# A hybrid conv/gMLP decoder layer in five matmul units: conv taps leave each unit's last row pair, y and z rows are prepared one pair sooner

## The chip, the cores and the metric

The kernel runs on one core of one Trainium2 chip. The metric is the device time of one execution in microseconds (us). The kernel before takes 1897.69 us (median of 3 runs, 1892.99 to 1901.14).

## The reference

The layer takes x of 4096 rows by 1024 columns in float32. Cut to what matters:

```python
h = layer_norm(x, ln_emb_g, ln_emb_b)
a_val, a_gate, a_z, b_u, b_v, b_z = split(h @ w_in, 6)          # 512 columns each
a = a_val * sigmoid(a_gate)
a = causal_depthwise_conv(a, conv_w, conv_b)                     # 31 taps per channel, along the rows
y_a = silu(layer_norm(a, conv_ln_g, conv_ln_b)) * silu(a_z)
v = layer_norm(gelu(b_v), sgu_ln_g, sgu_ln_b)                    # in chunks of 128 rows
sv = einsum("hts,bcshd->bcthd", tril(w_s), v) + b_s              # 8 heads, lower-triangular 128 x 128
y_b = gelu(b_u) * sv * silu(b_z)
z = layer_norm(ALPHA * h + concat(y_a, y_b) @ w_out, post_ln_g, post_ln_b)
out = z + sigmoid(z @ w_ple_gate + b_ple_gate) * (p @ w_ple)
```

## The kernel before

**Five units.** The work is five 1024 x 1024 products over all 4096 rows, one after the other, each called a unit: unit(0) makes a_val and a_gate, unit(1) b_u and b_v, unit(2) b_z and a_z, unit(3) the product with `w_out`, unit(4) the gate. The words of the change count them from one: its fourth unit is unit(3), its fifth unit(4). A unit runs over 16 pairs of 128 rows (`for p in range(NP)`, L427). A pair is one call of `group` (L325): a Strassen-like scheme that needs seven products of quarter blocks instead of eight, each product 12 matmuls of 128 x 512 (four blocks of the inner dimension, each as high times high, high times low, low times high part; L312 to L314). So a pair is 84 matmuls into the PSUM banks pa, pb, pd, pe. A VectorE or ScalarE instruction called `plus` (L328) moves an intermediate from one bank to another between the products, and TensorE cannot write the bank again before that instruction has read it.

**What is made beside the products.** For a product, a left operand is split into a high part (`ahi`, ScalarE, L231) and the rest (`alo`, POOL or VectorE, L232). A weight is loaded (`wst`, L414), and split into `whi` (ScalarE, L172) and `wlo` (VectorE, L173) in two halves; a unit has seven weights, thus 14 `wlo` instructions of 128 x 1024. The weights of the next unit are loaded and split during the last pair of a unit. In unit(3) and unit(4) the left operands come from rows that are first transposed by TensorE (`rows_left`, L245). The rows of y (L669) need a LayerNorm with six POOL instructions per pair (L691, L692, L694), the rows of z (L753) two multiplies and two adds of 128 x 1024 with the LayerNorm's gain and bias `prow`. The convolution (L365) runs on VectorE as 47 instructions, called taps here, for each of 16 blocks of 128 channels by 1024 rows; each tap reads one SBUF tile and a PSUM accumulator (L386, L392, L395).

**What sets the order.** The program is written with generators that are advanced a few steps at each of six places within a pair (`between`, L437): `bg` makes the left operands of the next pair, `bg_x` the rows of a later one, `bg_w` the weights, `bg_post` what follows a pair, and `bg_conv` the taps. At places 2 and 3 of every pair `bg_conv.step(conv_quota)` lets the quota of taps go: 6 in unit(0), 6 in unit(1), 10 in unit(2), 5 in unit(3), thus twice that in a pair. The order in which an engine's instructions finally stand is then set by the framework's scheduler; after that each engine works strictly in order, as does the queue of SP, which issues every DMA. A DMA whose data or buffer is not ready holds all later ones in SP's queue.

**Buffers.** Seven `big` buffers (8 KB per partition) hold weights in flight (`wst`), left operands before the split (`qa`, `qb`), rows of y, z and h, conv results (`cz`) and, from the end of unit(3) on, the pair of rows `prow`. Two `ca` buffers hold the convolution's input; after it they hold the bias row `gb` and the staging of `w_ple` (`wps`).

Of the kernel before, what the change touches and what calls it, by code (L numbers as in the profile page):

```python
# [8 lines left out]
F32 = mybir.dt.float32  # L9
# [3 lines left out]
ADD, SUB, MUL = ALU.add, ALU.subtract, ALU.mult  # L13
# [18 lines left out]
NP = S // (2 * P)  # L32
# [32 lines left out]
def hybrid_layer_kernel(  # L65
# [27 lines left out]
    pool = ctx.enter_context(tc.tile_pool(name="pool", bufs=1))  # L93
# [5 lines left out]
    def big(shape, name, dt=F32):  # L99
        return pool.tile(shape, dt, tag="big", name=name, bufs=7)  # L100
# [38 lines left out]
    def pair(t):  # L139
        return t.rearrange("j p d -> p j d")  # L140
# [35 lines left out]
    def combos(u):  # L176


        for c in range(4):
            q = big([P, 4, C], "bq")  # L180
            for i in range(2):
                for j in range(2):
                    dma(q[:, 2 * i + j], wq[u, i, j][:, c])
            yield
            for n, k in ((1, 0), (2, 2), (3, 3)):
                dma(twD[u][ROW[n]][:, c], q[:, k])
            ptt(q[:, 0], q[:, 1], q[:, 0], op=SUB)
            dma(twD[u][ROW[5]][:, c], q[:, 0])
            yield
            ptt(q[:, 1], q[:, 3], q[:, 1], op=SUB)  # L190
            dma(twD[u][ROW[7]][:, c], q[:, 1])
            yield
            ptt(q[:, 3], q[:, 3], q[:, 0], op=SUB)
            dma(twD[u][ROW[6]][:, c], q[:, 3])
            yield
            ptt(q[:, 2], q[:, 2], q[:, 3], op=SUB)
            dma(twD[u][ROW[4]][:, c], q[:, 2])
            yield
# [30 lines left out]
    def left(src, eng):  # L229
        hi, lo = atile("ahi"), atile("alo")  # L230
        act(hi, src, ID)  # L231
        eng.tensor_tensor(lo, src, hi.bitcast(F32), op=SUB)  # L232
        return hi, lo

    def left_kept(p, L):

        qa, qb = big([P, 4, C], "qa"), big([P, 3, C], "qb")
        dma(qa, qD[p][:, 0:4])
        dma(qb, qD[p][:, 4:7])
        yield  # L240
        for i, n in enumerate(ORDER):
            L[n] = left(quad((qa[:, i] if i < 4 else qb[:, i - 4])), nc.gpsimd)
            yield
# [162 lines left out]
    bg_x = Background()  # L406
    bg_w = Background()
    bg_conv = Background()
    bg_post = Background()

    def load_operands(u, W):
        for n in ORDER:
            stg = big([P, 4, C], "wst")
            dma(stg, twD[u][ROW[n]])  # L414
            W[n] = split_weight(stg)
            yield

    def broadcast(src, n, name, tile_of=big):
        t = tile_of([P, n, src.shape[-1]], name)
        for i in range(n):  # L420
            dma(t[:, i], src[i : i + 1, :].partition_broadcast(P))
        return t

    def unit(u, L, W, next_left, next_first, body, conv_quota, lag=0):


        for p in range(NP):  # L427
            Lnext, Wnext = {}, {}
            last = p + 1 == NP
            if not last:  # L430
                bg.add(next_left(p + 1, Lnext))
            elif next_first is not None:
                bg.add(next_first(Lnext))
                bg_w.drain()
                bg_w.add(load_operands(u + 1, Wnext))

            def between(i):  # L437
                bg_x.step(2 if lag else 1)
                if i >= lag:
                    bg.step(3 if lag else 2)  # L440
                bg_post.step(2)
                if last and u + 1 < 5:
                    bg_w.step(2 if i == 5 else 1)
                else:
                    bg_w.step(1)
                if i in (2, 3):
                    with tc.issue_after(anchor[0].ins):
                        bg_conv.step(conv_quota)

            body(p, L, W, between)  # L450
            bg.drain()
            bg_x.drain()
            if last:
                bg_w.drain()
                W = Wnext
            L = Lnext
        return L, W
# [39 lines left out]
    W = {}  # L497
# [4 lines left out]
    L = {}  # L502
# [51 lines left out]
    L, W = unit(0, L, W, left_a, lambda L: left_kept(0, L), body_a, 6)  # L554
# [65 lines left out]
        if p % 2 == 1:  # L620
            bg_post.add(mix(p // 2, V["g"], V["h"], V["l"]))

    L, W = unit(1, L, W, left_kept, lambda L: left_kept(0, L), body_b, 6)
    bg_post.drain()


    def body_c(p, L, W, between):
        if p == 1:
            bg_w.add(combos(3))
        if p == NP - 3:  # L630
            for i in range(2):
                cgb.append(broadcast(crow[i : i + 1, :], 1, "cgb", utile))
            load_y(0)
        elif p >= NP - 2:
            bg_x.add(y_rows(p - NP + 2))
        ua = big([P, 2, 2, C], "ua")
        us, az = ua[:, 0], ua[:, 1]
        dma(us, pair(uD[p // 2][2 * (p % 2) : 2 * (p % 2) + 2]))
        pa, pd = group(L, W, None, az[:, 0], az[:, 1], between)
        act(az, az, AF.Silu)  # L640
        dma(pair(azD[p]), az)
        for j, ps in ((0, pa), (1, pd)):
            zz = utile([P, C], "zz")
            act(zz, ps, AF.Silu)
            ptt(us[:, j], us[:, j], zz, op=MUL)
        dma(pair(ybD[p]), us)
        if p == NP - 2:
            load_y(1)
        elif p == NP - 1:
            load_h(0)  # L650
            load_y(2)
# [17 lines left out]
    def y_rows(p):  # L669
        cz, y = CZ.pop(p), Y[p]  # L670
        cc = flat(cz[:, 0]).rearrange("p (c j x) -> p c j x", c=CT, j=2)
        for j in (1, 0):
            tp = sbank("tc")
            for ct in range(CT):
                nc.tensor.transpose(
                    out=tp[:, ct * P : (ct + 1) * P],
                    in_=cc[:, ct, j],
                    identity=ident,
                )
            act(y[:, j, 0:C], tp, ID)  # L680
        yield
        mv = mvtile(2)
        for j in (1, 0):
            moments([y[:, j, 0:C]], mv[:, j, :])
        nb = scale_bias(mv)
        yield
        for j in (1, 0):
            ya = y[:, j, 0:C]
            act(ya, ya, ID, scale=mv[:, j, 1:2], bias=nb[:, j : j + 1])
            yield  # L690
            ptt(ya, ya, cgb[0][:, 0], op=MUL)  # L691
            ptt(ya, ya, cgb[1][:, 0], op=ADD)  # L692
            act(ya, ya, AF.Silu)
            ptt(ya, ya, cz[:, 1, j], op=MUL)  # L694
            yield

    def left_y(p, L):
        return rows_left(L, Y.pop(p))
# [2 lines left out]
        H[p] = big([P, 2, D], "hr")  # L701
        dma(H[p], pair(hT[p]))

    L, W = unit(2, L, W, left_kept, lambda L: left_y(0, L), body_c, 10)


    def z_out(p, z):
# [12 lines left out]
    def body_d(p, L, W, between):  # L720
        if p == 1:
            bg_w.add(combos(4))
        h = H.pop(p)
        if p + 1 < NP:
            load_h(p + 1)
        if p + 2 < NP:
            bg_x.add(y_rows(p + 2))
        if p + 2 >= NP:
            bg_x.add(z_rows(p + 2 - NP))
        z = big([P, 2, D], "z")  # L730
        pa, pd = group(
            L, W, [h[:, 0, 0:C], h[:, 0, C:], h[:, 1, 0:C], h[:, 1, C:]],
            z[:, 0, C:], z[:, 1, C:], between, scale=ALPHA,
        )
        for j, ps in ((0, pa), (1, pd)):
            act(z[:, j, 0:C], ps, ID)
        bg_post.drain()
        bg_post.add(z_out(p, z))
        if p + 3 < NP:
            load_y(p + 3)  # L740
        elif p + 3 == NP:
            pb_.append(broadcast(prow, 2, "prow"))
            load_z(0)
        elif p + 2 == NP:
            load_z(1)

    Z = {}

    def load_z(p):
        Z[p] = big([P, 2, D], "zr")  # L750
        dma(Z[p], pair(zT[p]))

    def z_rows(p):  # L753
        for j in (1, 0):
            ptt(Z[p][:, j], Z[p][:, j], pb_[0][:, 0], op=MUL)  # L755
            ptt(Z[p][:, j], Z[p][:, j], pb_[0][:, 1], op=ADD)  # L756
            yield

    pb_ = []
# [4 lines left out]
    def first_z(L):  # L764
        yield from left_z(0, L)

    L, W = unit(3, L, W, left_y, first_z, body_d, 5, 2)
    bg_post.drain()


    def row_tile(name):
        return pool.tile([P, D], F32, tag="ca", name=name, bufs=2)

    gb = row_tile("gb")
    dma(gb, grow.partition_broadcast(P))
    wp_hi, wp_lo = big([P, 2, D], "wph", F32R), big([P, 2, D], "wpl", F32R)

    def split_wp():
        for k in range(2):
            wps = row_tile("wps")  # L780
            dma(wps, wp[k])
            act(wp_hi[:, k], wps, ID)
            tt(wp_lo[:, k], wps, wp_hi[:, k].bitcast(F32), op=SUB)
# [105 lines left out]
```

## Time and profile before

| | |
|---|---|
| median of 3 runs | 1897.69 us |
| the profiled execution's own time | 1898.2 us |
| its span, first to last instruction | 1896.5 us |
| mean granted TensorE clock | 0.986 |
| busy share of the span: TensorE matmul / VectorE / POOL / ScalarE | 95% / 75% / 67% / 47% |
| DMA | 363.62 MB, mean 192 GB/s |

TensorE (PE) is busy nearly throughout, VectorE (DVE) and POOL for most of the time, and the DMA queues have room. The 92.5 us in which PE is idle (1896.5 less 1804.0 busy) are not spread evenly. The page cuts the span into 40 slices of 47 us and gives each engine's busy share in tenths. To see a stage more closely one asks for stretches. The pairs are found in the trace by counting matmuls, 84 to a pair: unit(1) starts at 401.06 us, unit(2) at 749.08, unit(3) at 1072.51, unit(4) at 1449.54. The stretches below run from the first matmul of one pair to the first of the next, so that their length is what the pair costs. In a stretch's row stand its length, then for each engine the busy us and the number of instructions, then the granted clock, the DMA share and the DMA rate.

### The profile page before, as it was taken

What the parts mean: (1) busy time and instruction counts of PE and PEld (TensorE: products, weight loads), DVE (VectorE), ACT (ScalarE), POOL (GpSimd) and SP (SyncE); (2) the same over time, 40 slices, a digit from 0 to 9 for tenths busy, and PEclk for the clock granted to TensorE, in tenths of its full rate; (3) what the DMA queues carried; (4) which work ended last, traced back from release to release, by engine and by line L of the source; (5) the groups of instructions that cost most, each with busy time, mean ns of one, the idle gap of its engine ahead of it and who ended that gap; (6) DMA issues with size and microseconds to landing.
All of it is one profiled execution on the core that took longest, in us unless ns stands there. A gap on an engine that the chain in (4) does not pass through costs nothing. (4 is left out here: it accounts for less than half of the span.)

```text
span 1896.5 us, 24392 instructions
## 1 busy us (share of the span) xinstructions
PE 1804.0 (95%) x8322; PEld 1470.9 (78%) x8322; DVE 1413.6 (75%) x2176; ACT 892.4 (47%) x1438; POOL 1269.9 (67%) x1015
## 2 busy tenths in 40 slices
PE   4799999999999999999999899999999999999999
PEld 3687788877788887788888677787887787888887
DVE  8637877797787778978787998887558856665654
ACT  4655555565455555544444634445555422332222
POOL 2878987458777676588668568757676856655541
PEclk9899999999999999999999889999999999999999
DMA  6579776586734445898666758745555322222311
GB/s 239 195 236 359 248 235 206 194 287 211 239 124 147 139 142 173 302 358 298 211 198 227 272 186 284 242 150 191 197 189 220 119 95 78 89 90 95 100 54 52
DMA packets 184940, 363.62 MB, mean 192 GB/s; under 512 B 49648, under 2 KB 74224, under 8 KB 177136
## 3 DMA queue, kind: packets, MB, share of 16 engines
q1 hardware_dynamic: 184816, 362.07, 55.3%
q8 instruction: 66, 1.08, 0.2%
q14 instruction: 58, 0.48, 0.1%
HBM read 211.02 MB, written 150.99 MB: 191 GB/s over the span
## 5 line engine op out<-in xcount | busy, mean ns | idle before, releaser
L232 POOL TENSOR_TENSOR alo<-s,ahi 128x512 fp32r<-128x512 f32 x192 | 262.8, 1382 | 260.7 <-ACT ahi L231 252.9
L312 PE MATMUL pb<-whi,ahi 128*128 128x512 f32 x960 | 385.9, 402 | 18.3 <-ACT pa L330 5.2
L313 PE MATMUL pb<-wlo,ahi 128*128 128x512 f32 x960 | 378.4, 394 | 1.6 <-DVE wlo L173 1.6
L314 PE MATMUL pb<-whi,alo 128*128 128x512 f32 x960 | 378.4, 394 | 0.1
L312 PE MATMUL pe<-whi,ahi 128*128 128x512 f32 x640 | 258.9, 405 | 19.6 <-ACT ahi L231 8.5
L314 PE MATMUL pe<-whi,alo 128*128 128x512 f32 x640 | 256.6, 401 | 2.1 <-POOL alo L232 2.1
L313 PE MATMUL pe<-wlo,ahi 128*128 128x512 f32 x640 | 254.6, 398 | 4.2 <-DVE wlo L173 4.2
L312 PEld LDWEIGHTS pb<-whi,ahi 128*128 128x128 f32 x960 | 182.3, 190 | 63.6 <-ACT pa L330 8.8
L314 PEld LDWEIGHTS pb<-whi,alo 128*128 128x128 f32 x960 | 182.1, 190 | 39.5 <-POOL alo L232 0.6
L313 PEld LDWEIGHTS pb<-wlo,ahi 128*128 128x128 f32 x960 | 182.7, 190 | 38.4 <-DVE wlo L173 2.6
L232 POOL TENSOR_TENSOR alo<-qa,ahi 128x512 fp32r<-128x512 f32 x128 | 171.2, 1353 | 48.1 <-ACT ahi L231 47.8
L231 ACT ACTIVATE ahi<-s 128x512 fp32r<-128x512 f32 x192 | 119.7, 629 | 138.9 <-DVE s L284 54.6
L386 DVE SCALAR_TENSOR_TENSOR acc<-ca,cs_sb,acc 128x512 f32<-128x512 f32 x240 | 180.1, 750 | 4.3
L395 DVE SCALAR_TENSOR_TENSOR acc<-ca,cw_sb,acc 128x512 f32<-128x512 f32 x240 | 179.0, 746 | 0.1
L392 DVE SCALAR_TENSOR_TENSOR acc<-zy,cw_sb,acc 128x512 f32<-128x512 f32 x224 | 166.8, 745 | 1.2 <-POOL zy L378 0.4
L312 PEld LDWEIGHTS pe<-whi,ahi 128*128 128x128 f32 x640 | 122.7, 192 | 47.1 <-ACT ahi L231 10.3
L232 POOL TENSOR_TENSOR alo<-qb,ahi 128x512 fp32r<-128x512 f32 x96 | 126.8, 1329 | 39.2 <-ACT ahi L231 38.2
L313 PEld LDWEIGHTS pe<-wlo,ahi 128*128 128x128 f32 x640 | 122.6, 191 | 30.4 <-DVE wlo L173 6.5
L232 DVE TENSOR_TENSOR alo<-tp,ahi 128x512 fp32r<-128x512 f32 x144 | 98.2, 683 | 62.9 <-ACT ahi L231 60.5
L314 PEld LDWEIGHTS pe<-whi,alo 128*128 128x128 f32 x640 | 122.3, 191 | 27.8 <-POOL alo L232 3.3
L312 PE MATMUL pd<-whi,ahi 128*128 128x512 f32 x320 | 129.4, 404 | 4.4 <-ACT pd L330 3.2
L159 POOL TENSOR_TENSOR mv<-mv,nhalf 128x2 f32<-128x2 f32 (+1 forms) x81 | 55.2, 687 | 111.2 <-DVE mv L158 110.3
(151 smaller groups left out, 4006.7 us busy)
## 6 DMA issues: line engine op xcount, KB each, us to landing
qa<-qD SPq DMA_DIRECT2D x32, 1024.0 KB, 6.5
twD<-bq SPq DMA_DIRECT2D x112, 256.0 KB, 5.7
wst<-twD SPq DMA_DIRECT2D x28, 1024.0 KB, 6.9
qb<-qD SPq DMA_DIRECT2D x32, 768.0 KB, 6.8
xr<-in_x SPq DMA_DIRECT2D x32, 512.0 KB, 5.4
hT<-xr SPq DMA_DIRECT2D x32, 512.0 KB, 3.8
qD<-s SPq DMA_DIRECT2D x64, 256.0 KB, 2.9
bq<-in_wq SPq DMA_DIRECT2D x64, 256.0 KB, 5.2
```

The source lines that it names most:

```text
L159: ptt(mv[:, :, 1], mv[:, :, 1], nhalf[:, 0:n], op=ALU.pow)
L231: act(hi, src, ID)
L232: eng.tensor_tensor(lo, src, hi.bitcast(F32), op=SUB)
L312: nc.tensor.matmul(ps, lhsT=ah[:, k, :], rhs=wh[:, k, :], start=start and k == 0, stop=False, **kw)
L313: nc.tensor.matmul(ps, lhsT=ah[:, k, :], rhs=wl[:, k, :], start=False, stop=False, **kw)
L314: nc.tensor.matmul(ps, lhsT=al[:, k, :], rhs=wh[:, k, :], start=False, stop=k == 3, **kw)
L386: stt(even, src, w, even, op0=MUL, op1=ADD)
L392: stt(dst, src, cw_sb[:, ct, 2 * k + 1 : 2 * k + 2], odd if k else even, op0=MUL, op1=ADD)
L395: stt(src if k == NE - 1 else even, src, cw_sb[:, ct, 2 * k : 2 * k + 1], even, op0=MUL, op1=ADD,)
```

## The change

Four things change, and with them the order on every engine.

1. `between` no longer lets taps go in the last pair of a unit. The quotas rise by one to make up for it: 7 in unit(1), 11 in unit(2), 6 in unit(3); unit(0) stays at 6.
2. In unit(2) the loads of y rows 0 and 1 and their preparation move one pair towards the front: `load_y(0)` and the `cgb` rows from the start of pair 13 to pair 12, `y_rows(0)` and `y_rows(1)` from pairs 14 and 15 to 13 and 14.
3. In unit(3) both `load_z(0)` and `load_z(1)` stand at the end of pair 13; `z_rows(0)` stays in pair 14 on POOL, `z_rows(1)` moves from pair 15 to pair 14 and from POOL to VectorE.
4. `prow` is loaded at pair 10 as two rows into the `ca` buffers, and `gb` and `wps` go to `big` buffers instead.

```diff
-                if i in (2, 3):
+                if i in (2, 3) and not last:
                     with tc.issue_after(anchor[0].ins):
                         bg_conv.step(conv_quota)
...
-    L, W = unit(1, L, W, left_kept, lambda L: left_kept(0, L), body_b, 6)
+    L, W = unit(1, L, W, left_kept, lambda L: left_kept(0, L), body_b, 7)
...
-        if p == NP - 3:
+        if p == NP - 4:
             for i in range(2):
                 cgb.append(broadcast(crow[i : i + 1, :], 1, "cgb", utile))
             load_y(0)
-        elif p >= NP - 2:
-            bg_x.add(y_rows(p - NP + 2))
+        elif p in (NP - 3, NP - 2):
+            bg_x.add(y_rows(p - NP + 3))
...
-        if p == NP - 2:
+        if p == NP - 3:
             load_y(1)
...
-    L, W = unit(2, L, W, left_kept, lambda L: left_y(0, L), body_c, 10)
+    L, W = unit(2, L, W, left_kept, lambda L: left_y(0, L), body_c, 11)
...
-        if p + 2 >= NP:
-            bg_x.add(z_rows(p + 2 - NP))
+        if p == 10:
+            for i in range(2):
+                pb_.append(row_tile("prow"))
+                dma(pb_[i], prow[i : i + 1, :].partition_broadcast(P))
+        if p + 2 == NP:
+            bg_x.add(z_rows(0))
+            bg_post.add(z_rows(1, nc.vector))
...
         elif p + 3 == NP:
-            pb_.append(broadcast(prow, 2, "prow"))
             load_z(0)
-        elif p + 2 == NP:
             load_z(1)
...
-    def z_rows(p):
+    def z_rows(p, eng=nc.gpsimd):
         for j in (1, 0):
-            ptt(Z[p][:, j], Z[p][:, j], pb_[0][:, 0], op=MUL)
-            ptt(Z[p][:, j], Z[p][:, j], pb_[0][:, 1], op=ADD)
+            eng.tensor_tensor(Z[p][:, j], Z[p][:, j], pb_[0], op=MUL)
+            eng.tensor_tensor(Z[p][:, j], Z[p][:, j], pb_[1], op=ADD)
             yield
...
-    L, W = unit(3, L, W, left_y, first_z, body_d, 5, 2)
+    L, W = unit(3, L, W, left_y, first_z, body_d, 6, 2)
...
-    gb = row_tile("gb")
+    gb = big([P, D], "gb")
...
-            wps = row_tile("wps")
+            wps = big([P, D], "wps")
```

The scheduler's order, counted pair by pair on VectorE (from one `L355` to the next), has these taps. Last pair of unit(0) and first of unit(1): 11 and 9 before, 6 and 6 now. Last of unit(1) and first of unit(2): 12 and 8, now 8 and 2. Pairs 14 and 15 of unit(2) and pair 0 of unit(3): 19, 16 and 14, now 21, 10 and 10. Pairs 1 to 10 of unit(3): 14, 11, 12, 8, 11, 12, 8, 12, 10, 1, now 8, 13, 10, 14, 15, 12, 2, 0, 0, 0. Pairs 1 to 14 of unit(1) hold 172 taps before and 196 now, pairs 1 to 14 of unit(2) 285 and 314. In unit(4)'s first pair the bias instruction `pa<-pb,gb`, without which TensorE can't go on in bank pb, stands behind 8 of the 14 `wlo` halves before and behind 13 now, and the load of `gb` behind the seventh weight's in SP's queue.

On VectorE, at the last pair of unit(2), where the weights of unit(3) are split (`wlo`) between taps (L386, L392, L395), before:

```order
L355 TENSOR_TENSOR ua<-pb,s_9619 128x512
L386 SCALAR_TENSOR_TENSOR acc<-ca,cs_sb,acc 128x512 x4
L173 TENSOR_TENSOR wlo<-wst,whi 128x1024
L392 SCALAR_TENSOR_TENSOR acc<-zy,cw_sb,acc 128x512
L395 SCALAR_TENSOR_TENSOR acc<-ca,cw_sb,acc 128x512
L173 TENSOR_TENSOR wlo<-wst,whi 128x1024
L392 SCALAR_TENSOR_TENSOR acc<-zy,cw_sb,acc 128x512
L274 TENSOR_TENSOR s_9843<-tp,a_9836 128x512
L395 SCALAR_TENSOR_TENSOR acc<-ca,cw_sb,acc 128x512
L392 SCALAR_TENSOR_TENSOR acc<-zy,cw_sb,acc 128x512
L395 SCALAR_TENSOR_TENSOR acc<-ca,cw_sb,acc 128x512
L392 SCALAR_TENSOR_TENSOR acc<-zy,cw_sb,acc 128x512
```

and at the same place now:

```order
L355 TENSOR_TENSOR ua<-pb,s_9692 128x512
L395 SCALAR_TENSOR_TENSOR ca<-ca,cw_sb,acc 128x512
L386 SCALAR_TENSOR_TENSOR acc<-ca,cs_sb,acc 128x512 x2
L173 TENSOR_TENSOR wlo<-wst,whi 128x1024
L386 SCALAR_TENSOR_TENSOR acc<-ca,cs_sb,acc 128x512
L173 TENSOR_TENSOR wlo<-wst,whi 128x1024
L386 SCALAR_TENSOR_TENSOR acc<-ca,cs_sb,acc 128x512
L274 TENSOR_TENSOR s_9911<-tp,a_9904 128x512
L386 SCALAR_TENSOR_TENSOR acc<-ca,cs_sb,acc 128x512
L173 TENSOR_TENSOR wlo<-wst,whi 128x1024
L386 SCALAR_TENSOR_TENSOR acc<-ca,cs_sb,acc 128x512
L173 TENSOR_TENSOR wlo<-wst,whi 128x1024
```

Fewer taps stand between the `wlo` halves, and the third and fourth half have moved up.

On SP's queue at the end of unit(1), where unit(2)'s weights (`wst`) are loaded; `cD` are the stores of a finished convolution block, which wait for its last taps, before:

```order
L239 DMA qb<-qD_109 128x1536
L414 DMA wst<-twD_174 128x2048
L401 DMA cD_130<-zy 1024x1x64
L414 DMA wst<-twD_174 128x2048
L401 DMA cD_130<-ca 1024x1x64
L414 DMA wst<-twD_174 128x2048
L375 DMA ca<-aD_126 128x2x15
L376 DMA ca<-aD_127 128x2x512
L414 DMA wst<-twD_174 128x2048 x4
```

and now:

```order
L401 DMA cD_130<-zy 1024x1x64
L401 DMA cD_130<-ca 1024x1x64
L375 DMA ca<-aD_126 128x2x15
L376 DMA ca<-aD_127 128x2x512
L238 DMA qa<-qD_109 128x2048
L239 DMA qb<-qD_109 128x1536
L586 DMA uD_139<-g_6582 128x4x512
L414 DMA wst<-twD_174 128x2048 x7
```

The conv block's stores have moved ahead of the weights, whose seven loads now stand together behind one other store (`uD`).

On VectorE in pair 14 of unit(3), where `pa` and `u` are the instructions that free bank pb, before:

```order
L334 SCALAR_TENSOR_TENSOR s_13288<-hr,pe 128x512
L334 SCALAR_TENSOR_TENSOR pa<-hr,pb 128x512
L232 TENSOR_TENSOR alo<-tp,ahi 128x512
L334 SCALAR_TENSOR_TENSOR u_13315<-hr,pb 128x512
L274 TENSOR_TENSOR s_13347<-tp,a_13340 128x512
```

and now, with line numbers of the changed kernel (L761 and L762 are the z rows' multiply and add):

```order
L334 SCALAR_TENSOR_TENSOR s_13291<-hr,pe 128x512
L761 TENSOR_TENSOR zr<-zr,prow 128x1024 x2
L232 TENSOR_TENSOR alo<-tp,ahi 128x512
L334 SCALAR_TENSOR_TENSOR pa<-hr,pb 128x512
L762 TENSOR_TENSOR zr<-zr,prow 128x1024 x2
L334 SCALAR_TENSOR_TENSOR u_13318<-hr,pb 128x512
```

Four instructions of 128 x 1024 have come in, two in front of each instruction that frees bank pb.

## Rows read from the trace of the kernel before

**Rows 1.** Busy tenths in 40 slices of the span, PE and VectorE.
```profile
PE   4799999999999999999999899999999999999999
DVE  8637877797787778978787998887558856665654
```

**Rows 2.** Stretches by pair, unit(2) pairs 13 to 15, unit(3) pair 0.
```profile
1007.97:1027.01 19.04, 19.04 (x86) 15.77 (x84) 15.12 (x24) 9.34 (x17) 15.91 (x14) 1.00 0.58 195
1027.01:1047.86 20.85, 20.85 (x101) 17.42 (x100) 17.47 (x28) 10.70 (x19) 18.64 (x18) 1.00 0.78 264
1047.86:1072.51 24.65, 21.88 (x94) 17.45 (x92) 24.32 (x26) 14.26 (x22) 12.46 (x10) 0.93 0.56 200
1072.51:1106.98 34.47, 27.43 (x104) 21.61 (x105) 33.10 (x41) 17.65 (x26) 15.43 (x12) 0.80 0.70 251
```

**Rows 3.** Timeline of PE: start, length, matmul, then idle before and its releaser.
```profile
1067.12 1.11 PE L257 MATMUL tp<-ident,y 128*128 128x128 f32 x4 [2.32 <-DVE alo L232]
...
1082.62 0.79 PE L312 MATMUL pb<-whi,ahi 128*128 128x512 f32 x1 [4.33 <-DVE ua L355]
```

**Rows 4.** Timeline of VectorE at the first weights of unit(3).
```profile
1052.62 7.50 DVE L173 TENSOR_TENSOR wlo<-wst,whi 128x1024 fp32r<-128x1024 f32 x1
1060.05 0.74 DVE L392 SCALAR_TENSOR_TENSOR acc<-zy,cw_sb,acc 128x512 f32<-128x512 f32 x1
1060.71 0.74 DVE L395 SCALAR_TENSOR_TENSOR acc<-ca,cw_sb,acc 128x512 f32<-128x512 f32 x1
1061.37 1.21 DVE L173 TENSOR_TENSOR wlo<-wst,whi 128x1024 fp32r<-128x1024 f32 x1
```

**Rows 5.** Timeline of POOL there, first and last of seven rows without a gap.
```profile
1047.73 2.54 POOL L691 TENSOR_TENSOR y<-y,cgb 128x512 f32<-128x512 f32 x2
...
1057.75 1.30 POOL L694 TENSOR_TENSOR y<-y,cz 128x512 f32<-128x512 f32 x1
```

**Rows 6.** Stretches by pair, unit(1) pairs 14 and 15, unit(2) pairs 0 and 1.
```profile
702.49:723.00 20.51, 20.51 (x98) 17.20 (x97) 16.40 (x27) 10.60 (x19) 15.42 (x15) 1.00 0.12 39
723.00:749.08 26.08, 24.02 (x109) 19.11 (x107) 20.65 (x38) 14.17 (x24) 16.48 (x15) 1.00 0.60 207
749.08:779.09 30.01, 24.12 (x102) 17.35 (x103) 27.74 (x35) 20.50 (x27) 10.61 (x10) 1.00 0.77 264
779.09:796.46 17.37, 17.37 (x78) 14.39 (x79) 16.02 (x27) 9.55 (x18) 16.40 (x14) 1.00 0.92 329
```

**Rows 7.** Timeline of SP's queue in pair 15 of unit(1).
```profile
735.62 0.32 SPq L414 DMA_DIRECT2D wst<-twD  x1
742.57 0.57 SPq L401 DMA_DIRECT2D cD<-zy  x1
744.01 0.32 SPq L414 DMA_DIRECT2D wst<-twD  x1
```

**Rows 8.** Two stretches of unit(3), pairs 1 to 9 and pairs 10 to 14.
```profile
1106.98:1318.55 211.57, 201.59 (x973) 163.75 (x972) 178.23 (x325) 103.38 (x162) 159.60 (x166) 0.99 0.64 216
1318.55:1428.38 109.83, 109.83 (x541) 90.55 (x540) 65.97 (x127) 55.18 (x88) 79.98 (x79) 1.00 0.55 192
```

**Rows 9.** Stretches by pair, unit(3) pair 15, unit(4) pairs 0, 1 and 7.
```profile
1428.38:1449.54 21.16, 20.73 (x95) 16.51 (x94) 17.25 (x19) 9.16 (x12) 16.24 (x10) 1.00 0.39 152
1449.54:1477.01 27.47, 23.28 (x101) 18.44 (x101) 25.66 (x30) 20.95 (x28) 15.33 (x9) 0.94 0.80 288
1477.01:1512.86 35.85, 31.21 (x132) 23.70 (x130) 28.27 (x31) 10.35 (x18) 29.23 (x14) 0.95 0.29 101
1646.07:1672.61 26.54, 26.54 (x126) 21.83 (x124) 17.61 (x23) 7.80 (x14) 16.00 (x10) 1.00 0.26 90
```

**Rows 10.** Timeline of PE in unit(4) pair 0.
```profile
1463.12 0.77 PE L312 MATMUL pb<-whi,ahi 128*128 128x512 f32 x1 [3.31 <-DVE pa L332]
```

**Rows 11.** Timeline of POOL in unit(3) pair 15, the rows of `z_rows(1)`.
```profile
1431.85 5.74 POOL L755 TENSOR_TENSOR zr<-zr,prow 128x1024 f32<-128x1024 f32 x2
1437.55 6.71 POOL L756 TENSOR_TENSOR zr<-zr,prow 128x1024 f32<-128x1024 f32 x2
```

More of the change, by code (lines that the diff above doesn't have):

```diff
@@ L741, in body_d, with row_tile @@
         elif p + 3 == NP:
-            pb_.append(broadcast(prow, 2, "prow"))
             load_z(0)
-        elif p + 2 == NP:
             load_z(1)
+    def row_tile(name):
+        return pool.tile([P, D], F32, tag="ca", name=name, bufs=2)
     Z = {}
@@ L765, in first_z @@
         yield from left_z(0, L)
-    L, W = unit(3, L, W, left_y, first_z, body_d, 5, 2)
+    L, W = unit(3, L, W, left_y, first_z, body_d, 6, 2)
     bg_post.drain()
-    def row_tile(name):
-        return pool.tile([P, D], F32, tag="ca", name=name, bufs=2)
-    gb = row_tile("gb")
+    gb = big([P, D], "gb")
     dma(gb, grow.partition_broadcast(P))
```

## The prediction

> **What bounds the kernel now.** I read the page's slices first, each 47.4 us. PE is at nine tenths or more nearly everywhere after the start; VectorE reaches nine in slices 9, 17, 23 and 24 and stands at eight among lower digits in 31 and 32, and these slices hold the starts of unit(1) to unit(4); in slice 23 PE dips [rows 1]. So nearly all of the span is matmul work that this change leaves as it is, and what can move lies around the changes of unit. Next come the stretches by pair, which price each change of unit against a quiet pair. A quiet pair of unit(2) costs 19.04 us [rows 2], of unit(1) 20.51 [rows 6], of unit(3) 109.83 / 5 = 21.97 [rows 8], of unit(4) 26.54 [rows 9]. Around the start of unit(3), pairs 14, 15 and 0 cost 20.85 + 24.65 + 34.47 = 79.97 against 19.04 + 19.04 + 21.97 = 60.05, an excess of 19.9 [rows 2, 8]. Around unit(2) it is 26.08 + 30.01 + 17.37 = 73.46 against 20.51 + 2 x 19.04 = 58.59, thus 14.9 [rows 6]. Around unit(4) it is 21.16 + 27.47 + 35.85 = 84.48 against 21.97 + 2 x 26.54 = 75.05, thus 9.4 [rows 9]. Pairs 1 to 9 of unit(3), which carry the rest of the convolution, cost 211.57 against 9 x 21.97, thus 13.8 [rows 8].
>
> Last come the waits inside the worst place. In pairs 15 and 0 around unit(3) VectorE is busy 24.32 of 24.65 and 33.10 of 34.47 us, and the granted clock is 0.93 and 0.80 [rows 2]: PE waits for VectorE, 2.32 us for an `alo` and 4.33 us for the `ua` that empties bank pb [rows 3], and the clock falls with the idling. VectorE's queue holds the weights' `wlo`, the taps and these small instructions, so each tap or slow `wlo` delays what PE waits for.
>
> **The change part by part.**
>
> *Start of unit(3): -10 us.* By the order, pairs 15 and 0 lose 10 of 30 taps and pair 14 gains 2. A tap takes 0.66 us from its start to the next one's (1060.71 to 1061.37) [rows 4], so 6.6 us leave VectorE where it is the bound, and 1.3 go to pair 14, where it has 3.4 us of room [rows 2]. The second gain is the y rows. The first `wlo` lasted 7.50 us, the next 1.21 [rows 4], and the long one ended 1.0 us after a gap-free run of POOL from 1047.73 to 1059.05, in which stand the six instructions on y row pair 1 [rows 5]. VectorE was held for 7.50 - 1.21 = 6.3 us. The change prepares y one pair sooner, so this run is over when the first `wlo` comes. Together 12.9 us of an excess of 19.9. I take 10, since a part of the excess is transposes on PE, and the weights' loads become the next limit. Bounds: -19.9 (all of it) and 0 (POOL is late by as much and meets `wlo` again).
>
> *Start of unit(2): -5 us.* Ten taps fewer in pairs 15 and 0 are 6.6 us, in a pair where VectorE is busy 27.74 of 30.01 [rows 4, 6]. On SP's queue the first weight was issued at 735.62 and the second at 744.01, behind a conv store at 742.57 that waited for its last tap [rows 7]; now all seven stand together, which can bring the second forward by up to 6.9 us, if a `big` buffer is free. The two overlap, and the weights still come through few buffers. Bounds -14.9 and 0.
>
> *Start of unit(1): -1 us.* Eight taps fewer are 5.3 us of VectorE. No row shows VectorE as the last wait there; bounds -5.3 and 0.
>
> *Unit(3) pairs 1 to 9: -3 us.* The excess of 13.8 fell on 98 taps, 0.14 us a tap; now there are 74, 24 fewer, -3.4. They are no thinner while they last (10.6 a pair against 10.9), the last two pairs become quiet. Bounds -13.8 and +3.
>
> *Inside unit(1) and unit(2): +1 us.* The quotas add some two taps a pair, 1.3 us. In unit(2) VectorE goes from 15.12 to 16.4 of 19.04 us [rows 2], in unit(1) from 16.40 to 17.7 of 20.51 [rows 6]: both are hidden beside matmuls. If that cover fails, VectorE is no better used than in unit(3), 178.23 of 211.57 or 84% [rows 8]: 16.4 / 0.842 = 19.5 and 17.7 / 0.842 = 21.0, thus 0.5 us a pair over 28 pairs, +13. Bounds 0 and +13, nearer to 0, since both pairs ran without an idle PE.
>
> *Start of unit(4): -3 us.* For: `prow` leaves the `big` buffers, so one more is free for weights, and pair 15 loses POOL's two multiplies and two adds, 5.74 + 6.71 = 12.45 us [rows 11], beside which `wlo` ran. Fewer `wlo` are then left for pairs 0 and 1, where VectorE was busy 25.66 of 27.47 [rows 9]. I take 5 of 9.4. Against: the first bias instruction now stands behind five `wlo` more, 5 x 1.21 = 6.1 us, and PE waited 3.31 us for it before [rows 10]; the weights must be early by that much. Against too: VectorE gets two multiplies and two adds of 128 x 1024 in pair 14. No row shows them on VectorE; the nearest is `wlo`, of the same size and also with two SBUF inputs: 1.21 alone, 7.50 under POOL [rows 4]. A bunch of two takes 2.4 us, while a product of 12 matmuls, which PE has in hand, takes 19.04 / 7 = 2.72. I charge 2 us, since POOL works on `z_rows(0)` then. Bounds -9.4 and, from the five `wlo` alone, +6. The moved loads (`load_z(1)`, `prow`) add nothing: the queue has them a pair earlier, and unit(3)'s quiet pairs run with a DMA share of 0.55 [rows 8].
>
> The Trainium skill bears on that 2 us ("SBUF — State Buffer", section "SBUF: two separate sides"): a VectorE instruction with two SBUF inputs and a POOL instruction exclude each other, whoever starts first for its whole length. By that a waiting instruction is held for one instruction of the other; the 6.3 us above, under instructions of about 1.3 us each, were several, so here the trace is harsher than the rule.
>
> *Sum.* -10 - 5 - 1 - 3 + 1 - 3 = -21 on the span of 1896.5, thus 1875.5; the profiled execution adds 1.7 around it (1898.2), 1877.2, and stands 0.5 over the median of the runs: about 1877 us.
>
> **The rivals.**
>
> *Loads bound the changes of unit (about 1892).* The taps were in nobody's way: a weight waits for its transfer and a free `big` buffer, and y and z rows held a pair longer take buffers away. For it: the 8.4 us between two weights' issues [rows 7]. Against: VectorE 97% busy in the two worst pairs [rows 2]. Then the start of unit(3) gains the 6.3 us of the held `wlo` and the other places nothing: 1897.7 - 6 = 1892.
>
> *The z rows on VectorE wait for one POOL instruction each (about 1886).* Each of the four waits out one on POOL, 5.74 / 2 = 2.87 [rows 11]: 4 x (1.21 + 2.87) = 16.3 us in two bunches, of which 2 x 2.72 are covered, a loss of 10.9 instead of 2: 1877 + 9 = 1886. This is what the exclusion of the skill's page above gives.
>
> *VectorE and POOL shut each other out for whole runs (about 1909, slower).* In pair 14 of unit(3) POOL has z and `alo` work back to back. The adds on VectorE stand in front of `pa` and `u`, both of which free the bank that PE writes next. If they are held for a run as `wlo` was, and this run has z rows in it, the wait is 11.3 [rows 5] + 12.45 [rows 11] = 23.7; plus 4.8 of their own, less 5.4 covered, that is 23; and if the first `wlo` after it is held once more, +6.3 [rows 4]. Against the other terms' -18 this gives +11, thus 1909. It decides against the change from a stall of 18 us on. For it: the 7.50. Against: `alo` on POOL waits for ScalarE now and then, so runs break.
>
> **How the numbers follow.** Forecast 0.60, loads 0.20, one-instruction waits 0.12, whole runs 0.08. About 0.5%, 9.5 us, is what a measurement of this kernel tells from no change; faster means below 1888.2, slower above 1907.2. The forecast lies below 1888 (own range 1861 to 1888), and so do two thirds of the one-instruction case: faster 0.60 + 0.08 = 0.68. Whole runs are the slower 0.08, and the middle holds the other 0.24. The range from 1860 to 1897 takes in the loads' case and the other mild one and leaves out whole runs and the sum of all lower bounds.
>
> **What would show it.** Right: the first `wlo` of unit(3) near 1.2 to 2.5 us; pairs 15 and 0 there below 23 and 28 us, with a granted clock near 1; unit(2)'s second weight issued within some 4 us of the first; unit(3) quiet from pair 8 on; pairs of unit(2) still at 19.04. Wrong: `zr` on VectorE far over 1.2 us with PE idle in front of bank pb in pair 14; PE waiting for `pa<-pb,gb` by more than the 3.31 of before; weights (`whi`) waiting for transfers at each change of unit as long as before; unit(2) pairs above 19.5.

## The result, and the profile after

The changed kernel takes 1911.75 us (median of 5 runs, 1909.7 to 1915.91) against 1897.69 of the kernel before (5 runs on the same chip): a ratio of 1.0074, 95% interval 1.0059 to 1.0088. It is slower by 0.74%, where 1877 was forecast, and lies above the forecast's range of 1860 to 1897. Its profiled execution took 1909.7 us with a span of 1908.0.

The stages, in us, from the matmul counts of the profiles. The second figure is a further execution of the same kernel (e5 and e6 below).

| stage | forecast | before | after | difference, first profiles |
|---|---|---|---|---|
| start of unit(1): last pair of unit(0), pair 0 | -1 | 45.9 / 45.3 | 46.6 / 48.4 | +0.8 |
| unit(1), pairs 1 to 14 | part of +1 | 296.6 / 296.2 | 307.2 / 303.4 | +10.6 |
| start of unit(2): pairs 15, 0, 1 | -5 | 73.5 / 71.9 | 73.2 / 76.6 | -0.3 |
| unit(2), pairs 2 to 13 | part of +1 | 230.5 / 230.5 | 232.7 / 233.4 | +2.2 |
| start of unit(3): pairs 14, 15, 0 | -10 | 80.0 / 79.2 | 69.2 / 69.1 | -10.8 |
| unit(3), pairs 1 to 13 | -3 (pairs 1 to 9) | 299.1 / 300.4 | 306.7 / 304.3 | +7.6 |
| start of unit(4): pairs 14, 15, 0, 1 | -3 | 106.7 / 106.8 | 109.8 / 112.5 | +3.1 |

Unit(0) gives back 1.3, so the differences come to +11.9, and the span grew by 11.5. One gain came in the size forecast, and three stages lost what was to be free or a gain. Two executions of one kernel differ by up to 3.7 us in a stage, so differences of that size in single profiles tell little.

The busy tenths of the changed kernel answer to [rows 1]; beside slice 23 PE now dips in slices 10 and 12 (unit(1)), 26 (unit(3)) and 31 (start of unit(4)):

```profile
PE   4799999998989999999999899899998999999999
DVE  8637987887778787988889977875568656556564
```

Stretches of the changed kernel: unit(1) pair 5; then, against [rows 6, 2, 8, 9], unit(1) pair 15, unit(2) pair 0, unit(2) pair 15, unit(3) pairs 0, 1 to 9 and 14, unit(4) pairs 0 and 1.

```profile
516.94:546.11 29.17, 23.53 (x99) 18.82 (x98) 22.42 (x33) 12.54 (x24) 22.65 (x20) 0.88 0.60 206
732.64:759.04 26.40, 24.91 (x119) 20.39 (x117) 16.98 (x34) 13.47 (x24) 15.54 (x17) 1.00 0.56 189
759.04:788.19 29.15, 24.16 (x103) 18.41 (x104) 27.68 (x35) 21.94 (x29) 8.43 (x7) 0.94 0.83 309
1057.57:1077.58 20.01, 20.01 (x93) 16.47 (x91) 19.97 (x25) 15.15 (x22) 9.43 (x7) 1.00 0.94 324
1077.58:1107.73 30.15, 24.70 (x106) 19.47 (x105) 27.43 (x34) 13.67 (x20) 13.34 (x10) 0.89 0.70 252
1107.73:1325.76 218.03, 206.28 (x973) 166.43 (x972) 160.80 (x300) 104.61 (x165) 159.41 (x165) 0.97 0.60 209
1414.44:1442.56 28.12, 23.83 (x112) 19.29 (x110) 22.56 (x29) 10.35 (x17) 25.76 (x17) 0.94 0.41 158
1462.67:1495.66 32.99, 25.43 (x104) 20.40 (x103) 27.35 (x32) 21.46 (x27) 20.75 (x11) 0.84 0.63 245
1495.66:1524.27 28.61, 27.41 (x129) 22.48 (x127) 18.57 (x25) 8.39 (x15) 17.47 (x9) 1.00 0.34 120
```

**Unit(1), pair 5.** The largest single loss: 29.17 us against 19.77 for the same pair before. The stretch of that pair and VectorE's multiply L602 in it, before:

```profile
518.52:538.29 19.77, 19.39 (x97) 16.11 (x95) 15.27 (x25) 12.35 (x24) 18.32 (x17) 1.00 0.58 202
...
525.06 1.06 DVE L602 TENSOR_TENSOR v<-v,sgb 128x512 f32<-128x512 f32 x1
```

Timeline of all engines there in the changed kernel (an idle time in brackets names what ended it):

```profile
523.66 1.32 POOL L232 TENSOR_TENSOR alo<-qa,ahi 128x512 fp32r<-128x512 f32 x1
...
524.61 4.62 DVE L602 TENSOR_TENSOR v<-v,sgb 128x512 f32<-128x512 f32 x1 [1.38 <-ACT v L601]
524.91 3.77 POOL L232 TENSOR_TENSOR alo<-qb,ahi 128x512 fp32r<-128x512 f32 x3
...
529.81 0.68 DVE L603 TENSOR_TENSOR v<-v,sgb 128x512 f32<-128x512 f32 x1
...
530.52 0.63 ACT L604 ACTIVATE vh<-v 128x512 fp32r<-128x512 f32 x1 [5.94 <-DVE v L603]
...
532.01 0.60 ACT L330 ACTIVATE s<-pe 128x512 f32<-128x512 f32 x1
...
532.66 0.80 PE L312 MATMUL pe<-whi,ahi 128*128 128x512 f32 x1 [5.64 <-ACT s L330]
```

It is to be read backwards. PE waits 5.64 us for ScalarE's `s`. ScalarE had stood 5.94 us at `vh`, which is ahead of `s` in its queue, for VectorE's `v`. And VectorE's multiply L602 took 4.62 us, where L603 takes 0.68: it ended at 529.23, 0.55 us after POOL's run of `alo` (524.91 + 3.77 = 528.68), so its own work seems to have begun when the run was over. A second L602, in pair 2, took 3.34 us. Of the 9.4 us lost, 5.3 are idle time of PE (5.64 against 0.38), and 4.1 are busy time: 23.53 us for 99 matmuls at a granted clock of 0.88, against 19.39 for 97 at 1.00.

**Start of unit(3).** The held `wlo` of [rows 4] is gone, the first two are:

```profile
1061.93 1.48 DVE L173 TENSOR_TENSOR wlo<-wst,whi 128x1024 fp32r<-128x1024 f32 x1
...
1063.99 1.78 DVE L173 TENSOR_TENSOR wlo<-wst,whi 128x1024 fp32r<-128x1024 f32 x1
```

**Start of unit(2).** SP's queue, which answers to [rows 7], and from the waits of that queue between 728 and 776 us what held `wst` (us in total, times, longest):

```profile
744.74 0.37 SPq L586 DMA_DIRECT2D uD<-g  x1
753.10 22.21 SPq L414 DMA_DIRECT2D wst<-twD  x7
```
```profile
SPq L414 <- DMA uD<-g: 7.9, 1, 7.9
```

The seven weights do stand together now, but the first is issued at 753.10, 5.9 us ahead of the unit's first matmul; before it was 749.08 - 735.62 = 13.5 ahead. It waited 7.9 us for the store `uD`, whose source holds the buffer that it needs. The second weight now follows 1.55 us behind the first, but 4.4 us ahead of the unit's first matmul, where it was 5.1 ahead before: it came forward by nothing, since the first went back.

**Unit(3), pair 2.** PE's queue and SP's:

```profile
1133.80 0.82 SPq L183 DMA_DIRECT2D bq<-in_wq  x2
1135.14 1.66 SPq L183 DMA_DIRECT2D bq<-in_wq  x2
1136.85 0.52 SPq L660 DMA_DIRECT2D cz<-cD  x1
...
1143.65 1.09 PE L675 MATMUL tc<-ident,cz 128*128 128x128 f32 x4 [3.27 <-DMA cz<-cD]
```

PE waits for a convolution result `cz`, whose load stands behind the loads `bq` for unit(4)'s weights (`combos(4)`). No tap is in these rows. The wait is 3.27 of the 12.3 us for which PE idles in pairs 1 to 13; others there are 2.53 us for an `alo` of POOL and 2.8 us in four waits for an `ahi` of ScalarE.

**Start of unit(4).** The stretch of pair 14 of unit(3) before, then, in the changed kernel, that pair and pair 0 of unit(4):

```profile
1406.12:1428.38 22.26, 22.26 (x111) 18.01 (x110) 14.22 (x25) 10.46 (x17) 20.93 (x16) 1.00 0.68 246
...
1424.04 4.03 DVE L761 TENSOR_TENSOR zr<-zr,prow 128x1024 f32<-128x1024 f32 x2 [1.40 <-DMA zr<-zT]
1427.99 0.68 DVE L232 TENSOR_TENSOR alo<-tp,ahi 128x512 fp32r<-128x512 f32 x1
...
1428.77 1.09 PE L257 MATMUL tp<-ident,y 128*128 128x128 f32 x4 [4.29 <-issue]
1429.18 5.08 DVE L762 TENSOR_TENSOR zr<-zr,prow 128x1024 f32<-128x1024 f32 x2
...
1468.66 6.79 DVE L173 TENSOR_TENSOR wlo<-wst,whi 128x1024 fp32r<-128x1024 f32 x4
...
1475.98 0.67 DVE L232 TENSOR_TENSOR alo<-tp,ahi 128x512 fp32r<-128x512 f32 x1
...
1476.70 1.97 PE L257 MATMUL tp<-ident,zr 128*128 128x128 f32 x8 [4.77 <-DVE alo L232]
...
1481.46 0.80 PE L312 MATMUL pb<-whi,ahi 128*128 128x512 f32 x1 [2.78 <-DVE pa L332]
```

The four instructions on z rows take 4.03 + 5.08 = 9.1 us, and PE stands 4.29 us before the transposes `tp`. Their row names no releaser; the `alo` queued behind the first two, which reads the bank `tp`, ended 0.1 us earlier. In pair 0 four `wlo` in a row do the same (4.77). The wait for the bias instruction, now behind the 13th `wlo`, is 2.78, where it was 3.31 before [rows 10]. Pair 0 loses 5.5, pair 14 5.9, and pair 1 gets 7.2 back.

### The profile page after: what moved, and what is told of

The parts are those of the page before. It is cut to its first block, busy times and chain, and to the rows that moved or that the text cites. A ratio compares the mean times of both kernels' runs of the same rounds, so it can differ in the third digit from the quotient of the medians.

```text
span 1908.0 us, 24398 instructions
## 1 busy us (share of the span) xinstructions
PE 1806.7 (95%) x8322; PEld 1475.7 (77%) x8322; DVE 1416.1 (74%) x2180; ACT 891.9 (47%) x1438; POOL 1256.8 (66%) x1011
## 4 chain that ended last, share of the span: by engine, by line
PE 49%; DVE 8%; DMA 6%; POOL 4%; issue 3%; ACT 2%; SPq 0%; POOLq 0%; DVEq 0%; ACTq 0%
PE pb L312 6%; PE pb L314 6%; PE pb L313 6%; PE pe L314 4%; PE pe L312 4%; PE pe L313 4%; PE pp L808 4%; PE pd L312 2%; PE tp L257 2%; PE pa L314 2%; PE pa L312 2%; PE pd L313 2%; PE pa L313 2%; PE pd L314 2%; POOL alo L232 2%
## 5 line engine op out<-in xcount | busy, mean ns | idle before, releaser
L386 DVE SCALAR_TENSOR_TENSOR acc<-ca,cs_sb,acc 128x512 f32<-128x512 f32 x240 | 180.0, 750 | 3.8
L395 DVE SCALAR_TENSOR_TENSOR acc<-ca,cw_sb,acc 128x512 f32<-128x512 f32 x240 | 178.8, 745 | 0.4 <-POOL ca L379 0.3
L392 DVE SCALAR_TENSOR_TENSOR acc<-zy,cw_sb,acc 128x512 f32<-128x512 f32 x224 | 166.7, 744 | 2.9 <-POOL zy L378 2.0
```

Of the source, the lines that this page charges most:

```text
L386: stt(even, src, w, even, op0=MUL, op1=ADD)
L392: stt(dst, src, cw_sb[:, ct, 2 * k + 1 : 2 * k + 2], odd if k else even, op0=MUL, op1=ADD)
L395: stt(src if k == NE - 1 else even, src, cw_sb[:, ct, 2 * k : 2 * k + 1], even, op0=MUL, op1=ADD,)
```

## The experiments

Ratios are to the kernel before on the same chip, with 95% intervals; e5, e6, e8 and e11 were executed once and have none.

**e1: taps and y rows alone.** The first two parts without the higher quotas.

```diff
 before.py
-                if i in (2, 3):
+                if i in (2, 3) and not last:
 (and y rows one pair sooner, as in the change)
```

> The kernel before with two parts alone: no taps in the last pair of a unit, and y rows one pair sooner; quotas stay 6, 10 and 5, the z rows as before. Theory A (the start of unit(3) gains by these two parts, and the losses belong to the quotas and the z rows): start of unit(3) near 69 us against 80, the rest as before, about 1887 us. Rival B (taps taken out of the last pairs must be done elsewhere, and cost there what they saved): unit(3) pairs 1 to 13 longer by 8 us or more, about 1896 us.

Measured: 1928.43 us, ratio 1.0158 (1.012 to 1.0195). Both theories missed the size. The 44 taps that the last pairs no longer take don't fit into five a place any more, and what is left when `load_y(12)` needs the last block is let go at once: 45 taps in pair 10 of unit(3). The timeline of PE and the stretch of that pair:

```profile
1366.15 1.94 PE L675 MATMUL tc<-ident,cz 128*128 128x128 f32 x8 [20.72 <-DMA cz<-cD]
```
```profile
1320.91:1373.19 52.28, 27.58 (x121) 21.61 (x120) 43.68 (x71) 7.30 (x14) 10.22 (x9) 0.80 0.33 112
```

So the higher quotas are no free choice: the taps have a due time. The start of unit(3) did gain (73.2 against 80.0). And unit(1) lost 6.4 us with its quota left at 6 and 168 taps in pairs 1 to 14 against 172, and with no L602 or L603 above 1.9 us: neither more taps nor a long hold can be the reason there, and which it is stays open.

**e2: the quotas alone.** Before, with 7, 11 and 6.

> The kernel before with the higher quotas alone (7, 11, 6). Rival R (seven taps are too much VectorE work in unit(1)): pairs 1 to 14 of unit(1) take 306 us or more against 296.6, about 1907 us. Theory H (in the changed kernel one multiply by sgb was held by a run of POOL instructions, which is a matter of what happens to meet): no loss of that size in unit(1) unless a long L602 or L603 shows again; 1890 to 1900 us.

Measured: 1905.64 us, ratio 1.0029 (1.0015 to 1.0043); unit(1) 301.7, between the two theories. Of its 5.2 us more, none lies in pairs 6 to 14, which with 124 taps against 108 take 183.5 us against 184.7; all lies in pairs 1 to 5, beside `combos(2)`, where L602 took at most 2.58 us. Here only 39 taps are left for unit(3) from pair 1 on, before it was 99. Yet its pairs 1 to 13 take 304.1 us against 299.1, so the number of taps isn't what that stage pays for. The start of unit(3) took 73.5 us, though taps run in unit(2)'s last pair and the y rows are where they were before. Its first `wlo`:

```profile
1060.43 1.30 DVE L173 TENSOR_TENSOR wlo<-wst,whi 128x1024 fp32r<-128x1024 f32 x1
```

**e3: the z rows' parts alone.** The changed kernel with the first two parts and the quotas undone.

> The kernel before with the z rows' parts alone (both z loads at pair 13, z_rows(1) on VectorE in pair 14, prow in the ca buffers, gb and wps in big buffers); taps, quotas and y rows as before. Theory A: pairs 14 and 15 of unit(3) and 0 and 1 of unit(4) cost some 3 us more than before, as in the changed kernel (109.8 against 106.7), about 1901 us. Rival: the loss came with the other parts, and this one gains the 3 us that were forecast, about 1895 us.

Measured: 1900.15 us, ratio 1.001 (0.9995 to 1.0025): no difference that can be told. By its profile theory A: pairs 14 to 1 take 110.1 us against 106.7. The start of unit(3), untouched, took 75.5 in place of 80.0, but pairs 1 to 13 of unit(3) took 3.2 us more, so the whole time doesn't show it. VectorE's `wlo` there:

```profile
1053.06 2.21 DVE L173 TENSOR_TENSOR wlo<-wst,whi 128x1024 fp32r<-128x1024 f32 x1
1056.52 2.24 DVE L173 TENSOR_TENSOR wlo<-wst,whi 128x1024 fp32r<-128x1024 f32 x1
```

With the same instructions around it as before, the first `wlo` began 1.45 us after POOL's L692 in place of 1.14 (1052.62 - 1051.48 before), and waited for what was left of one POOL instruction, not for a run.

**e4: one SBUF tile in place of two.** The changed kernel with

```diff
-            tt(v, v, sgb[0][:, 0], op=MUL)
+            nc.vector.tensor_scalar(v, v, sgb[0][:, 0, 0:1], None, op0=MUL)
 (the add likewise)
```

> The changed kernel, in which the multiply and the add by the rows sgb in unit(1) take one scalar per partition in place of the row (so gain and bias of that LayerNorm are wrong): the same two VectorE instructions of 128 x 512, but with one SBUF tile as input in place of two. Theory H (the two-input instruction was shut out while POOL ran): no L602 or L603 above 1.7 us, pair 5 of unit(1) near 20 us, pairs 1 to 14 of unit(1) near 298 us, about 1902 us. Rival R (VectorE has too much to do with quota 7): unit(1) stays near 307 us, about 1911 us.

Measured: 1904.46 us, ratio 1.0025 (1.0008 to 1.0042); unit(1) 296.2. The time is near what theory H gave, its reason is not shown by it: the instruction alone now takes 0.45 us, where it took 0.68, so the chain got shorter in every pair, and in pair 5 it was held all the same (27.0 us for the pair):

```profile
521.04 4.40 DVE L602 TENSOR_SCALAR v<-v,sgb 128x512 f32<-128x512 f32 x1 [0.44 <-ACT v L601]
```

An instruction with one SBUF input can be shut out too. The run doesn't decide between H and R.

**e5 and e6: both kernels once more.**

> The kernel before once more, for a second profile of the same instructions. Theory V (the held wlo of 7.50 us in the first profile was a chance of that execution): no wlo above 4 us at the start of unit(3), pairs 14, 15 and 0 there near 75.5 us, as in the run that left unit(2) as it is (75.50), while pairs 1 to 14 of unit(1) stay within 3 us of 296.6. Rival S (it belongs to the order): a wlo of some 7 us again and 80 us for the three pairs.

> The changed kernel once more, for a second profile. If the loss belongs to the order of its instructions: pairs 1 to 14 of unit(1) again near 307 us, with an L602 of 4 us or more in pair 5 and 29 us for that pair; pair 14 of unit(3) again near 28 us. If it is chance: pair 5 near 20 us, unit(1) near 298.

Measured: 1899.16 and 1913.06 us. VectorE in e5, then in e6:

```profile
1052.35 7.52 DVE L173 TENSOR_TENSOR wlo<-wst,whi 128x1024 fp32r<-128x1024 f32 x1 [0.36 <-ACT whi L172]
```
```profile
523.48 4.66 DVE L602 TENSOR_TENSOR v<-v,sgb 128x512 f32<-128x512 f32 x1
```

Both long holds come again at their places, and pair 5 takes 28.9 us: S holds, and the loss belongs to the order. (Unit(1) as a whole took 303.4 us in place of the 307 named. And e3 shows that a slightly later arrival can still undo such a hold.) The long L602 of pair 5 stands in the other two runs that leave unit(1) as in the changed kernel too: 4.63 us in e10, 4.64 in e11.

**e8: POOL's load in unit(1) taken away.** The changed kernel without the four subtractions per chunk of `combos(2)`:

```diff
-            ptt(q[:, 0], q[:, 1], q[:, 0], op=SUB)
+            if u != 2: ptt(q[:, 0], q[:, 1], q[:, 0], op=SUB)
 (the other three likewise)
```

> The changed kernel, in which POOL leaves out the 16 subtractions that prepare unit(2)'s weights during pairs 1 to 6 of unit(1) (so those weights are wrong; their transfers stay). VectorE has the same instructions and taps in every pair. Theory H (POOL's runs hold VectorE's v<-v,sgb): no L602 or L603 above 2 us, pair 5 near 21 us, pairs 1 to 14 of unit(1) near 298 us, about 1902. Rival R (VectorE's own load, or the phase of the convolution): unit(1) near 305 us or more, about 1910.

Measured: 1907.47 us; unit(1) 295.0. VectorE's taps are the same number in every pair of unit(1) as in the changed kernel. VectorE's multiply in pair 5, and the pair:

```profile
521.74 1.68 DVE L602 TENSOR_TENSOR v<-v,sgb 128x512 f32<-128x512 f32 x1
```
```profile
515.58:536.16 20.58, 20.58 (x97) 17.13 (x96) 17.94 (x30) 11.66 (x21) 16.59 (x17) 1.00 0.62 218
```

Theory H: with 196 taps and POOL's runs cut short, the 10 us are gone, so R falls. What the kernel before would gain without these subtractions wasn't run. (The whole time is only 2.2 us under that of the changed kernel's first profile, 1909.7: the start of unit(2) took 78.1 here in place of 73.2, and pair 14 of unit(3) to the end 3.1 more.)

**e10 and e9: combos(4) later.** The changed kernel (e10), and e7 (e9), each with

```diff
-        if p == 1:
+        if p == 6:
             bg_w.add(combos(4))
```

> The changed kernel with combos(4) from pair 6 of unit(3) on. Theory C: pairs 1 to 13 fall from 304 to 307 to about 299 us, no wait for cz above 2 us in pairs 1 to 3, about 1905 us. Rival D: about the same 304 to 307 us, 1911 us. Rival T (the taps, 8 to 15 a pair in pairs 1 to 6, make the excess): as D, since the taps stay.

> The kernel with no taps in the last pair of unit(2) alone (quota 11 there) and y rows sooner, in which moreover the preparation of unit(4)'s weights (combos(4): bq loads, POOL subtractions, stores) starts in pair 6 of unit(3) in place of pair 1. Theory C (in pairs 1 to 5 of unit(3) PE waits for cz, whose load stands among the bq loads and stores in SP's queue and shares the transfers with them): pairs 1 to 13 fall from 303.3 to about 296 us, PE's idle time there from 10.5 to under 5, about 1885 us. Rival D (the waits move along with combos(4) to pairs 6 to 10, where taps still run): 302 us or more, about 1892 us.

Measured: e10 1904.22 us, ratio 1.0032 (1.0016 to 1.0047); pairs 1 to 13 298.5. e9 1895.34 us, ratio 0.9991 (0.9979 to 1.0004); pairs 1 to 13 304.9. PE's longest wait for `cz` in e10 and the two longest in e9:

```profile
1255.67 1.09 PE L675 MATMUL tc<-ident,cz 128*128 128x128 f32 x4 [4.32 <-DMA cz<-cD]
```
```profile
1253.83 1.94 PE L675 MATMUL tc<-ident,cz 128*128 128x128 f32 x8 [5.04 <-DMA cz<-cD]
...
1280.05 0.63 PE L675 MATMUL tc<-ident,cz 128*128 128x128 f32 x4 [2.52 <-DMA cz<-cD]
```

In both the wait for `cz` left pairs 2 to 4 and came again where combos(4) had gone, in pair 7 (e10) and pairs 7 to 9 (e9). The load itself is slower there. Median us from issue to landing, last in the row: changed kernel, pairs 2 to 4; e10, pairs 2 and 3; e10, pairs 7 to 9:

```profile
cz<-cD SPq DMA_DIRECT2D x3, 512.0 KB, 6.7
cz<-cD SPq DMA_DIRECT2D x3, 512.0 KB, 3.4
cz<-cD SPq DMA_DIRECT2D x3, 512.0 KB, 7.1
```

So the collision is shown, and the taps alone, which stayed, were not it (T falls). Its price goes with the place: e10 got 6 to 8 us, as theory C, e9 nothing, as rival D. Taps still run through pairs 6 to 9 in e9 and end in pair 7 in e10; whether combos(4) costs by itself or only beside taps was not separated.

**e11: z_rows(0) left out.** The changed kernel without the line `bg_x.add(z_rows(0))`.

> The changed kernel, in which POOL leaves out the two multiplies and two adds of z_rows(0) (so the first rows of unit(4) lack gain and bias). VectorE still has the four instructions on z_rows(1) in pair 14 of unit(3). Theory H (they are long since POOL works beside them): the two multiplies take about 2.4 us in place of 4.03 and the two adds 2.4 in place of 5.08, PE waits under 2 us, pair 14 takes about 23 us. Rival W (their own length and the place in front of alo, pa and u make the wait): 3 us of PE idle or more and 26 us or more for the pair.

Measured: 1908.16 us; pair 14 22.3 us, PE's longest wait in it 0.68. VectorE's four:

```profile
1424.15 3.45 DVE L760 TENSOR_TENSOR zr<-zr,prow 128x1024 f32<-128x1024 f32 x2
...
1428.12 2.35 DVE L761 TENSOR_TENSOR zr<-zr,prow 128x1024 f32<-128x1024 f32 x2
```

Theory H: 5.8 us in place of 9.1, and the whole loss of the pair is gone. The first two still met one `alo` on POOL. The order moved as well: VectorE's `alo`, between the two bunches in the changed kernel, now stands behind both, so the run doesn't separate the shorter instructions from the new place of `alo`.

**e7: what gains, alone.** Taps leave the last pair of unit(2) only, its quota is 11, y rows come sooner; the rest as before.

```diff
 before.py
-                if i in (2, 3):
+                if i in (2, 3) and not (last and u == 2):
...
-    L, W = unit(2, L, W, left_kept, lambda L: left_y(0, L), body_c, 10)
+    L, W = unit(2, L, W, left_kept, lambda L: left_y(0, L), body_c, 11)
 (and y rows one pair sooner, as in the change)
```

> The kernel before with no taps in the last pair of unit(2) alone, quota 11 there, and y rows one pair sooner; unit(0) and unit(1) word for word as before, quotas 6, 6, 5, z rows as before. Theory A (the gain sits at the start of unit(3), the losses in unit(1) and in the z rows): units 0 and 1 as before, start of unit(3) near 70 us, unit(3) pairs 1 to 13 near 299, start of unit(4) near 106: about 1888 us, or 1892 if only 75.5 of the 80 us there are typical. Rival B (whatever is moved costs elsewhere what it gains): unit(3) pairs 1 to 13 near 306, no change, 1896 to 1900 us.

Measured: 1891.71 us (12 runs), ratio 0.9955 (0.9938 to 0.9972): by little, but faster than the kernel before. Unit(1) stays at 297.0, the start of unit(3) takes 73.7, pairs 1 to 13 303.3, so between A and B. The start of unit(4) takes 99.0 us against 106.7, pairs 2 to 15 of unit(4) 389.4 against 383.6; from pair 14 of unit(3) to the last of these matmuls it takes 482.5 us against 484.5.

## Why the prediction was wrong

*Start of unit(3), -10: right in size.* Measured -10.8 and -10.1, with the first `wlo` at 1.48 us, as named, and pair 15 at 20.0. Pair 0 took 30.15 at a clock of 0.89, where under 28 and near 1 were named; pair 14, back at a quiet 19.0, made up for it. The hold that is gone was in both profiles of before. The split into 6.6 us for taps and 6.3 for the y rows is not shown: e1 and e7, which have both parts, gained 6.8 and 6.3 us in all, and e2 and e3, in which the y rows stay and taps run in the last pair, lost the hold too (first `wlo` 1.30 and 2.21 us) and gained 6.5 and 4.5. Only pair 14 goes with these two parts in every run: 19.0 us with them, 20.9 without. So the size of this term owes something to luck.

*Inside unit(1) and unit(2), +1: the step that failed most.* Unit(1) alone took 10.6 us more. The 24 taps more were costed as VectorE time that is hidden beside matmuls, and in the quiet pairs so they were: pairs 6 to 10 took 101.4 us against 102.6, with 70 taps against 60 and no idle PE in either. What was missing: with the taps, all that follows in the queues moves, and a small instruction on PE's path may then meet a run of POOL. I had found this mechanism at one `wlo`, had kept it as the rival of whole runs, and had placed it in pair 14 of unit(3) alone. It struck at L602 in pair 5 of unit(1), for 9.4 us. The rival's 1909 is near the measured time, but its path was another: no stall of 18 us in pair 14, so that nearness is luck. Smaller waits of the same chain (ScalarE's `pa` behind `vh`) also grew in pairs 1 to 3, from 1.2 and 1.6 us to 3.5, 1.2 and 3.9, but another wait there, 3.8 us before, went, and the three pairs took 70.9 us against 70.3. By e1 and e2 unit(1) can also lose 5 to 6 us without a long hold; which shift of the order brings that is not settled. Unit(2) stayed near the forecast: 2.2 us over twelve pairs.

*Unit(3) pairs 1 to 9, -3: wrong in kind.* Measured +6.5. "The excess of 13.8 fell on 98 taps" was a coincidence in time: 39 or 74 taps in place of 99 left the excess as large. The last pairs did become quiet, as named, but the pairs before them cost more. With combos(4) moved away the changed kernel got 6 to 8 us back with the same 74 taps (e10), so a part of the excess belongs to combos(4). By the profiles PE's waits for `cz` are only some of it: 1.0 of 9.9 us of idle PE in the first profile of before (3.2 with one that ended together with a VectorE instruction), 5.0 of 12.5 in e5, 3.3 of 12.3 in the changed kernel, 8.0 of 10.4 in e7. What makes up the rest stays open.

*Start of unit(2), -5: wrong, by its own condition.* The second weight did follow the first within 4 us, as named, and nothing was gained by it. "If a `big` buffer is free": it wasn't, for 7.9 us. Here the rival that loads bound the changes of unit fits. e1, e2 and e7, with and without taps in that last pair, all lie between 71.6 and 75.3, as the kernel before does (73.5 and 71.9).

*Start of unit(4), -3: wrong sign.* The 2 us for the z rows on VectorE became 5.9 in pair 14: 9.1 us of VectorE in place of the 4.8 assumed, beside POOL's own z rows (e11). Pair 0 lost 5.5 us, near the 6.1 set against it for the five `wlo`, but by another wait: PE stood 4.77 us for an `alo` behind four `wlo`, and the bias instruction kept it for no longer than before. Pair 1 gave 7.2 back.

## What to carry to other kernels

Before costing an added instruction at nothing because its engine has room, follow the chain of small instructions that frees PE's next bank, and ask what will stand ahead of each in its queue after the shift; in this kernel a gap-free run on POOL was a danger wherever a VectorE instruction with two SBUF inputs came to meet it (4.62 us in place of 0.68, 7.50 in place of 1.21). Work that is taken out of a crowded place has a due time elsewhere: here 45 taps fell due at once, and one pair took 52.3 us in place of 21.9. Take apart a change of several parts by running each alone: two of the parts, kept to unit(2), make the kernel 0.45% faster, all together 0.74% slower.

## What the hardware showed that was not expected

How long VectorE is shut out by POOL changed with tenths of a us in its arrival. The same `wlo` before the same POOL run took 7.50 and 7.52 us (before, e5; begun 1.14 and 1.11 us after L692) and 2.21 (e3; 1.45 us after). Counted over the trace of before: of some 60 `wlo`, `sgb` and `zr` instructions that began while a POOL instruction of over 0.6 us ran with another right behind it, all but three waited no longer than for what was left of that one; in the changed kernel it was all but four of some 55. The Trainium skill ("SBUF — State Buffer", section "SBUF: two separate sides") says that whoever starts first has the ports for the whole instruction. By these counts the trace agrees in all but a few cases, and one of the few costs 4 to 6 us.

The few are alike. Over all thirteen traces 36 of 731 such instructions were held longer, each by 1 us or more, and 35 of the 36 had begun within the last 0.5 us of the POOL instruction (225 began so late, 506 earlier). Why some of these are passed over again and most aren't stays open.

The same section of the Trainium skill names, beside two SBUF inputs, VectorE instructions in a two-port mode. With e4's row (0.45 us alone, 4.40 held) the trace agrees, if its shorter time is that mode, which no row shows: fewer operands were no way round.
